# Two sums of a Strassen group, from VectorE additions to adding transfers

## The chip, the core and the metric

The kernel runs on one core of a Trainium2 chip. A core has TensorE (matrix products; PE and, for its weight loads, PEld in the profile), VectorE (DVE), ScalarE (ACT), GpSimd (POOL) and SyncE (SP), each with its own queue of instructions worked off in order, and DMA transfers that engines issue and that then run by themselves. Two kinds matter here: loads issued from SP, and loads and adding transfers issued from POOL. An adding transfer reads one region and adds it onto another where that lies. The metric is the device time of the launch in microseconds (us).

## The reference

One block of an encoder on 256 rows of 2048 numbers, in float32: a gated feed-forward part, an attention and a retention mixer side by side, a second feed-forward part, a last normalisation. The change lies in the first feed-forward part:

```python
def rmsnorm(x, g):
    y = xf * lax.rsqrt(jnp.mean(xf * xf, axis=-1, keepdims=True) + EPS)
    return (y * g.astype(jnp.float32)).astype(x.dtype)

def swiglu_ffn(x, w_gate, w_up, w_down):
    return (jax.nn.silu(x @ w_gate) * (x @ w_up)) @ w_down

x = x + 0.5 * swiglu_ffn(rmsnorm(x, norm_ffn1_g[l]), ffn1_w_gate[l], ffn1_w_up[l], ffn1_w_down[l])
...
x = x + merged @ w_out[l]
x = x + 0.5 * swiglu_ffn(rmsnorm(x, norm_ffn2_g[l]), ffn2_w_gate[l], ffn2_w_up[l], ffn2_w_down[l])
return rmsnorm(x, norm_final_g)
```

The gate and up matrices are 2048 x 5632, the down matrix 5632 x 2048.

## The kernel before

**Products.** Every float32 factor is split into a high part and a low remainder, and a product is three matrix products: high by high, high weight by low activation, low weight by high activation. A chunk of weights is 256 rows by 512 columns, 128 partitions by 1024 numbers. `split` (lines 132 to 136) makes its halves: ScalarE copies it to the high half (L134), VectorE subtracts that from the chunk for the low half (L135). `three` issues the products at L145, L146 (with the high half) and L148 (with the low half). Four split chunks can be alive at a time, and five raw ones.

**Strassen groups.** The gate and up products of one block of 512 columns are made together, as a two by two block product with seven products of sums in place of eight (class `Strassen`, L524). Each group is named after the entry at which it begins: `z10` is the first one, `z46` the second. It works on four chunks `jc` = 0 to 3 in four phases. For the first phase it loads, over POOL's queue, tiles `z10k` (up) and `z10x` (gate) for each chunk (`go`, L552). The plain halves `hiz1000r` to `loz1003r` are split from `z10k`; then the *first sum* of each chunk, `x = x + k`, is made and split into `hiz1000s` to `loz1003s`. In a name like `loz1003s` the last digits are the phase (0), the chunk (3), and `r` for a plain chunk or `s` for a sum. The second phase adds a further raw chunk onto `x` (L608), splits the sum, then forms `k = x - k` (L593) and lets an adding transfer put another chunk onto `x` (`third`, L594).

**Who makes the first sums.** `first` (L541) does it on VectorE, in place. For chunks named in `group.added`, `add_on` (L557) issues an adding transfer from `k` onto `x` on POOL's queue instead, `add_wait` entries after the chunk's second load. `weave` (L698) gives each group `group.added = group.added[:n]` with `n` its number in its part: none for group 0, chunk 0 for group 1, chunks 0 and 1 for the later ones.

**The order of the work.** The program is a written list of entries, each one chunk or a pair of a plain chunk and a sum; `run` walks it, preparing chunks some entries ahead. `later(n, ...)` puts something n entries behind. `kept.extend` (L729) releases the eight loads of the first group one entry apart. All of it is fixed when the program is built: on each engine the instructions stand in one order, and each waits for what it reads.

**The start.** The first ten entries ahead of `z10` are ordinary gate and up chunks (`acc`, names `hi`, `lo`, `raw`). While they run, VectorE and ScalarE also form the sums of the normalised activations that the groups need (`n1s5`, `n1s6`, `n1s3`, `n1s7`; L494 to L508), and ScalarE the squares of the norm (`n1sq`, L436). The norm's factor `n1rstd` (L383) is made on POOL.

Of the kernel before, what the change touches and what calls it, by code (L numbers as in the profile page):

```python
# [41 lines left out]
RET_WAIT = (14, 5)  # L42
HELD = 6
MIX_ADDED = (0,)
HEAD_AT = (3, 6, 10, 13, 17, 20, 24, 27)

MIX_SHARE = (0.5,) * 4 + (1.0,) * 4 + (0.0,) * 4 + (0.2,) * 4
# [33 lines left out]
def block_kernel(ctx: ExitStack, tc: tile.TileContext, x, g1, w1g, w1u, w1d, gm, w_in, rel, woa, wor, wo,  # L81
# [32 lines left out]
    def later(n, fn):  # L114
        due.setdefault(state["step"] + n, []).append(fn)
# [34 lines left out]
    def standard(job, k0):  # L150

        made = {}
        c = len(steps)

        parts = [slice(j, j + 1) for j in range(KC)] if c == 0 else [slice(0, KC)]

        def load():
            made["raw"] = weights_tile(f"raw{c}")
            fetch(made["raw"], job.w, job.rows[k0], job.col0, parts)

        def prep():
            if c > 0:
                made["hl"] = split(made.pop("raw"), c)
                return

            hi, lo = made["hl"] = split_tiles(c)
            raw = made.pop("raw")
            for p in parts:
                nc.vector.tensor_copy(hi[:, p, :], raw[:, p, :])
            first_low.extend(lambda p=p: nc.vector.tensor_sub(lo[:, p, :], raw[:, p, :], hi[:, p, :].bitcast(F32)) for p in parts)  # L170

        def products(only=None):
            if k0 == 0 and only in (None, 0) and not job.seed:
                open_banks(job)
            hi, lo = made["hl"]
            turns = [
                [
                    (
                        job.acc[part], job.act(k0 + j, t), (hi[:, j, cs], lo[:, j, cs]),
                        k0 + j == 0 and not job.seed, k0 + j == job.nk - 1,  # L180
                    )
                    for j in range(KC)
                ]
                for part, (t, cs) in enumerate(job.parts) if only in (None, part)
            ]

            if 0 < k0 < job.nk - KC:
                turns = [sum(turns, [])]
            for products in turns:
                three(products, bool(job.seed))  # L190
            if only is None and k0 + KC == job.nk:
                close(job)

        return Step(job, k0, load, prep, ("raw",), products)
# [503 lines left out]
    def weave(jobs, apart, groups, lead, share, start=None, extra=0):  # L698


        queue = [(job, k) for job in jobs for k in range(0, job.nk, KC)]
        at_hand = {}

        def next_standard():

            if len(queue) <= apart:
                return False
            job, k = queue[0]
            if any(at_hand.get(b, len(steps) + 1) > len(steps) for b in job.needs):
                return False  # L710
            steps.append(standard(job, k))
            del queue[0]
            if job.makes is not None and k + KC == job.nk:
                at_hand[job.makes] = len(steps) + 9
            return True

        for _ in range(lead):
            next_standard()
        seconds = []
        rate = (len(queue) - apart) / (len(groups) * sum(share))  # L720
        credit = 0.0
        first = max(len(steps) - 8, D // NB)
        for n, (b, make) in enumerate(groups.items()):
            group = make()
            group.added = group.added[:n]
            loads = group.loads()
            if start is not None and n == 0:
                loads[0] = lambda load=loads[0]: [start(), load()]
            kept.extend((first + i if n == 0 else 0, fn) for i, fn in enumerate(loads))  # L729
            for i, part in enumerate(group.steps()):  # L730
                if i == HALF_K // KC + 2:
                    seconds.append(len(steps))
                steps.extend(part)
                credit += rate * share[i]
                if i + 1 == len(share):
                    at_hand[b] = len(steps) + 7

                turn = i + 1 == 3 * (HALF_K // KC)
                if (turn or credit >= (0.2 if (i + 1) % (HALF_K // KC) == 0 else 0.6)) and next_standard():
                    credit -= 1  # L740
        if extra:
            due.setdefault(seconds[0], []).append(lambda: room.update(kept=room["kept"] + extra))
            due.setdefault(len(steps), []).append(lambda: room.update(kept=room["kept"] - extra))
        for job, k in queue:
            steps.append(standard(job, k))

    def ffn(name, norm, wg, wu, wd, after, start=None):
# [83 lines left out]
        for job, follow in zip(jobs, jobs[1:]):  # L831
            job.next = follow
        groups = {b: (lambda b=b: paired(b)) for b in range(nblocks) if b != PLAIN}
        weave(jobs, len(downs[PASSES[-1]]) * len(PASSES[-1]) * 4 // KC + HELD, groups, LEAD[start is None], SHARE, start, EXTRA)


# [169 lines left out]
    def all_attention():  # L1006
        for h in range(HEADS):
            for s, stage in attention(h):
                later(HEAD_AT[h] + s, stage)

# [67 lines left out]
    def gates(col1, col2, func, dsts):  # L1078
# [9 lines left out]

        return Strassen(nm, w_in0, col1, w_in0, col2, evict, MIX_ADDED)

# [6 lines left out]
    def queries():  # L1097
# [9 lines left out]

        return Strassen(nm, w_in0, QA, w_in0, QA + NB, evict, MIX_ADDED)

    groups = {"qa": queries, **groups}  # L1110
    weave(
        [proj(KA + b * NB, att_qk_done("ka", b), both) for b in range(2)]
        + [proj(VA + b * NB, nat_done("va", b, AF.Copy), both) for b in range(2)]
# [215 lines left out]
```

## Time and profile before

| | before |
|---|---|
| median of 3 runs | 2052.51 us (2051.78 to 2052.53) |
| the profiled execution, its own time | 2052.5 us |
| its span | 2050.7 us |
| PE busy | 2033.1 us (99%) |
| PEld busy | 1678.2 us (82%) |
| DVE busy | 1789.2 us (87%) |
| ACT busy | 1499.5 us (73%) |
| POOL busy | 343.8 us (17%) |
| granted TensorE clock, mean | 0.999 |

1.8 us of the profiled execution lie outside its span. PE's busy time comes from modelled ends of pipelined products, so gaps are better read from the weight loads (PEld): each product needs one, and where a load waits, a bracket behind its row says how long the engine was idle and for whom.

### The profile page before, as it was taken

Reading aid. Unit: us, or ns where it says so; the run is one execution under the profiler, and the core shown is the slowest. Engines: PE = TensorE matmul, PEld = TensorE weight load, DVE = VectorE, ACT = ScalarE, POOL = GpSimd, SP = SyncE. Lnnn points to the kernel's source line nnn. Section 1 sums busy time; section 2 is a strip of 40 time slices with the busy share of each in tenths; the row PEclk is TensorE's granted clock in tenths of the full one; section 3 lists DMA queues with packets and bytes.
Section 4 is the critical chain, followed back from the end, with each engine's and each line's share of the span. In section 5 each row is a group of like instructions: output and inputs, shape, how many; then the busy total and the mean of one; then the engine's idle time right before and its main releaser. Section 6 shows DMA issues by size and latency. Waiting matters only on the chain.

```text
span 2050.7 us, 26315 instructions
## 1 busy us (share of the span) xinstructions
PE 2033.1 (99%) x9188; PEld 1678.2 (82%) x9188; DVE 1789.2 (87%) x1837; ACT 1499.5 (73%) x1890; POOL 343.8 (17%) x403
## 2 busy tenths in 40 slices
PE   9999999999999999999999999999999999999998
PEld 7788888888888878888888888888788888888886
DVE  7999999999998799999987667569989999989996
ACT  7788888878787767777775434556788788888785
POOL 1221122212112022112120000011212221112200
PEclk9999999999999999999999999999999999999999
DMA  8888889988878679899896645576989988889974
GB/s 289 246 249 259 253 269 283 260 243 246 262 233 270 223 214 300 280 280 286 251 324 221 222 139 190 185 241 187 271 263 270 275 245 234 268 258 269 277 205 134
DMA packets 226853, 506.33 MB, mean 247 GB/s; under 512 B 15824, under 2 KB 16576, under 8 KB 226720
## 3 DMA queue, kind: packets, MB, share of 16 engines
q1 hardware_dynamic: 154560, 297.31, 43.1%
q0 software_dynamic: 67952, 198.36, 37.0%
q10 hardware_dynamic: 4208, 8.99, 1.2%
q8 instruction: 72, 1.18, 0.2%
q14 instruction: 61, 0.50, 0.1%
HBM read 472.08 MB, written 12.06 MB: 236 GB/s over the span
## 4 chain that ended last, share of the span: by engine, by line
PE 93%; DVE 3%; DMA 2%; ACT 1%; issue 1%; POOL 0%; SPq 0%; DVEq 0%; POOLq 0%; ACTq 0%
PE acc L148 15%; PE acc L145 15%; PE acc L146 15%; DMA z1030k<-in_ffn_w_up_dram 1%; DMA raw<-in_ffn_w_gate_dram 1%; DMA z1030x<-z1030k 1%; DVE lo L135 1%; PE z425a L145 0%; PE z777a L145 0%; PE z704a L146 0%; PE z958a L145 0%; PE z262a L145 0%; PE z190a L145 0%; PE z425a L146 0%; PE z226a L146 0%
## 5 line engine op out<-in xcount | busy, mean ns | idle before, releaser
L135 DVE TENSOR_TENSOR lo<-raw,hi 128x1024 fp32r<-128x1024 f32 x351 | 427.0, 1219 | 118.0 <-ACT hi L134 115.2
L134 ACT CAST hi<-raw 128x1024 fp32r<-128x1024 f32 x351 | 367.7, 1050 | 161.0 <-PE acc L146 125.7
L817 ACT ACTIVATE xall<-acc 128x512 f32<-128x512 f32 x160 | 94.5, 590 | 13.6 <-PE acc L148 9.7
L814 ACT ACTIVATE acc<-xall 128x512 f32<-128x512 f32 x160 | 95.9, 599 | 2.5
L145 PE MATMUL acc<-hi,mgh 128*128 128x512 f32 x128 | 50.2, 392 | 0.0
L146 PE MATMUL acc<-hi,mgl 128*128 128x512 f32 x128 | 49.8, 389 | 0.0
L148 PE MATMUL acc<-lo,mgh 128*128 128x512 f32 x128 | 35.5, 389 | 0.0
L145 PE MATMUL acc<-hi,nma01h 128*128 128x512 f32 x80 | 32.5, 407 | 0.0
L145 PE MATMUL acc<-hi,nma00h 128*128 128x512 f32 x80 | 32.3, 404 | 0.0
L146 PE MATMUL acc<-hi,nma01l 128*128 128x512 f32 x80 | 31.3, 391 | 0.0
L146 PE MATMUL acc<-hi,nma11l 128*128 128x512 f32 x80 | 31.3, 391 | 0.0
L146 PE MATMUL acc<-hi,nma00l 128*128 128x512 f32 x80 | 31.2, 390 | 0.0
L145 PE MATMUL acc<-hi,nma11h 128*128 128x512 f32 x80 | 31.2, 390 | 0.0
L146 PE MATMUL acc<-hi,nma10l 128*128 128x512 f32 x80 | 31.2, 390 | 0.0
L145 PE MATMUL acc<-hi,nma10h 128*128 128x512 f32 x80 | 31.2, 390 | 0.0
L148 PEld LDWEIGHTS acc<-lo,mgh 128*128 128x128 f32 x128 | 24.0, 188 | 5.0
L145 PEld LDWEIGHTS acc<-hi,mgh 128*128 128x128 f32 x128 | 24.0, 188 | 4.9
L146 PEld LDWEIGHTS acc<-hi,mgl 128*128 128x128 f32 x128 | 24.0, 188 | 4.8
L145 PE MATMUL acc<-hi,atth 128*128 128x512 f32 x64 | 26.2, 410 | 0.0
L148 PE MATMUL acc<-lo,nma01h 128*128 128x512 f32 x80 | 24.9, 393 | 0.6 <-DVE lo L135 0.6
L145 PE MATMUL acc<-hi,reth 128*128 128x512 f32 x64 | 25.3, 395 | 0.0
L146 PE MATMUL acc<-hi,attl 128*128 128x512 f32 x64 | 25.1, 392 | 0.0
(6884 smaller groups left out, 7258.8 us busy)
## 6 DMA issues: line engine op xcount, KB each, us to landing
raw<-in_ffn_w_down_dram SPq DMA_DIRECT2D x176, 512.0 KB, 6.7
raw<-in_w_in_dram SPq DMA_DIRECT2D x80, 512.0 KB, 5.0
raw<-in_w_out_dram SPq DMA_DIRECT2D x32, 512.0 KB, 4.1
raw<-in_ffn_w_up_dram SPq DMA_DIRECT2D x16, 512.0 KB, 5.0
raw<-in_w_out_att_dram SPq DMA_DIRECT2D x16, 512.0 KB, 4.3
raw<-in_w_out_ret_dram SPq DMA_DIRECT2D x16, 512.0 KB, 3.9
raw<-in_ffn_w_gate_dram SPq DMA_DIRECT2D x15, 512.0 KB, 4.9
z390x<-in_w_in_dram POOLq DMA_DIRECT2D x8, 512.0 KB, 8.7
```

The source lines that it names most:

```text
L134: nc.scalar.copy(hi, raw)
L135: nc.vector.tensor_sub(lo, raw, hi.bitcast(F32))
L145: nc.tensor.matmul(acc, ahi, whi, start=first, stop=False, **more)
L146: nc.tensor.matmul(acc, alo, whi, start=False, stop=False, **more)
L148: nc.tensor.matmul(acc, ahi, wlo, start=False, stop=last, **more)
L814: nc.scalar.activation(acc, xs[t][:, cols], AF.Copy, scale=2.0)
L817: nc.scalar.activation(xs[t][:, cols], acc, AF.Copy, scale=0.5)
```

## The change

The last two first sums of group `z10` are taken from VectorE and made by adding transfers. `add_wait` is set to 2 for this group, so the transfer for a chunk is called for two entries after the chunk's `x` load. The chunks 0 and 1 stay on VectorE. Other groups are as before.

```diff
@@ -42,6 +42,7 @@
 HELD = 6
 MIX_ADDED = (0,)
+FIRST_ADDED = (2, 3)
 HEAD_AT = (3, 6, 10, 13, 17, 20, 24, 27)
@@ -722,7 +723,9 @@
         for n, (b, make) in enumerate(groups.items()):
             group = make()
-            group.added = group.added[:n]
+            group.added = FIRST_ADDED if n == 0 and start is not None else group.added[:n]
+            if n == 0 and start is not None:
+                group.add_wait = 2
             loads = group.loads()
```

Only the first feed-forward part passes a `start`. The new line shifts line numbers by one, and by three from L726 on.

On POOL's queue, at the first group's loads, before (`z10k_435` and `z10x_463` are chunk 2, `z10k_487` and `z10x_503` chunk 3; a name behind the arrow is what is read):

```order
L552 DMA z10k_435<-in_ffn_w_up_dram 128x2x512
L552 DMA z10x_463<-in_ffn_w_gate_dram 128x2x512
L552 DMA z10k_487<-in_ffn_w_up_dram 128x2x512
L552 DMA z10x_503<-in_ffn_w_gate_dram 128x2x512
L383 TENSOR_TENSOR n1rstd<-v,mhalf 128x2
L594 DMA z10x_340<-in_ffn_w_up_dram 128x2x512
```

and after:

```order
L553 DMA z10k_435<-in_ffn_w_up_dram 128x2x512
L553 DMA z10x_463<-in_ffn_w_gate_dram 128x2x512
L553 DMA z10k_487<-in_ffn_w_up_dram 128x2x512
L553 DMA z10x_503<-in_ffn_w_gate_dram 128x2x512
L558 DMA z10x_463<-z10k_435 128x1024
L558 DMA z10x_503<-z10k_487 128x1024
L384 TENSOR_TENSOR n1rstd<-v,mhalf 128x2
L595 DMA z10x_340<-in_ffn_w_up_dram 128x2x512
```

The two adding transfers stand behind all eight loads and ahead of the norm's factor. Both wait there until the two loads of their chunk have landed.

On VectorE, at the plain halves and sums of the first phase, before:

```order
L135 TENSOR_TENSOR loz1002r<-z10k_435,hiz1002r 128x1024
L541 TENSOR_TENSOR z10x_463<-z10x_463,z10k_435 128x1024
L503 TENSOR_TENSOR n1f_258<-n1x_158 128x4x128
L508 TENSOR_TENSOR n1s3l<-n1f_258,n1s3h 128x512
L135 TENSOR_TENSOR loz1001s<-z10x_411,hiz1001s 128x1024
L500 SCALAR_TENSOR_TENSOR n1f_397<-n1f_397,n1x_348 128x4x128
L508 TENSOR_TENSOR n1s6l<-n1f_397,n1s6h 128x512
L135 TENSOR_TENSOR loz1003r<-z10k_487,hiz1003r 128x1024
L541 TENSOR_TENSOR z10x_503<-z10x_503,z10k_487 128x1024
L135 TENSOR_TENSOR lo_559<-raw_325,hi_558 128x1024
L508 TENSOR_TENSOR n1s7l<-n1f_258,n1s7h 128x512
L135 TENSOR_TENSOR loz1002s<-z10x_463,hiz1002s 128x1024
```

and after:

```order
L136 TENSOR_TENSOR loz1002r<-z10k_435,hiz1002r 128x1024
L504 TENSOR_TENSOR n1f_258<-n1x_158 128x4x128
L509 TENSOR_TENSOR n1s3l<-n1f_258,n1s3h 128x512
L136 TENSOR_TENSOR loz1001s<-z10x_411,hiz1001s 128x1024
L501 SCALAR_TENSOR_TENSOR n1f_397<-n1f_397,n1x_348 128x4x128
L509 TENSOR_TENSOR n1s6l<-n1f_397,n1s6h 128x512
L136 TENSOR_TENSOR loz1003r<-z10k_487,hiz1003r 128x1024
L136 TENSOR_TENSOR lo_559<-raw_325,hi_558 128x1024
L509 TENSOR_TENSOR n1s7l<-n1f_258,n1s7h 128x512
L136 TENSOR_TENSOR loz1002s<-z10x_463,hiz1002s 128x1024
```

Two additions are gone and nothing else has moved. TensorE's, ScalarE's and SyncE's rows stand in the same order in both programs; ScalarE's `hiz1002s` and `hiz1003s` now wait for the adding transfers where they waited for VectorE.

## The prediction, as put on record before the changed kernel ran

> **What bounds the kernel now.** I first read the table of busy time by windows of 50 us, over the whole span, to see where TensorE is not full. Columns: window, length, busy us and count for PE, PEld, DVE, ACT, POOL, granted clock, DMA share, GB/s; ahead of it the page's line of busy time.
>
> ```profile
> PE 2033.1 (99%) x9188; PEld 1678.2 (82%) x9188; DVE 1789.2 (87%) x1837; ACT 1499.5 (73%) x1890; POOL 343.8 (17%) x403
> 0.00:50.00 50.00, 48.13 (x213) 37.93 (x214) 37.17 (x47) 39.05 (x70) 7.49 (x15) 1.00 0.83 296
> 50.00:100.00 50.00, 47.99 (x208) 37.44 (x208) 49.46 (x52) 35.99 (x44) 14.27 (x16) 1.00 0.83 232
> 100.00:150.00 50.00, 50.00 (x226) 41.45 (x226) 47.59 (x44) 40.42 (x52) 10.93 (x12) 1.00 0.87 250
> 600.00:650.00 50.00, 50.00 (x222) 41.40 (x221) 46.28 (x44) 40.11 (x51) 8.24 (x9) 1.00 0.79 221
> ```
>
> From 100 to 650 us PE is full in every window (the first and the last of eleven are shown). In the window from 50 to 100 us, where group z10 is worked on, PE does 208 products in place of some 226, and VectorE is busy for 49.46 of 50 us. The clock is 1.00, so this is no throttling. Next, the weight loads in time order for that stretch, those rows that carry a wait, and the two loads ahead of the largest.
>
> ```profile
> 49.84 0.30 PEld L148 LDWEIGHTS z10a<-loz1003r,n1a00h 128*128 128x128 f32 x2 [0.20 <-DVE loz1003r L135]
> 54.77 0.19 PEld L145 LDWEIGHTS z10c<-hiz1003s,n1s5h 128*128 128x128 f32 x1
> 55.00 0.19 PEld L146 LDWEIGHTS z10c<-hiz1003s,n1s5l 128*128 128x128 f32 x1
> 56.46 0.30 PEld L148 LDWEIGHTS z10c<-loz1003s,n1s5h 128*128 128x128 f32 x2 [1.27 <-DVE loz1003s L135]
> 73.02 0.30 PEld L148 LDWEIGHTS z10c<-loz1013r,n1s3h 128*128 128x128 f32 x2 [0.31 <-DVE loz1013r L135]
> 75.29 0.30 PEld L148 LDWEIGHTS acc<-lo,n1a01h 128*128 128x128 f32 x2 [1.04 <-DVE lo L135]
> 80.96 0.30 PEld L148 LDWEIGHTS z10b<-loz1020r,n1a01h 128*128 128x128 f32 x2 [0.37 <-DVE loz1020r L135]
> 81.63 0.42 PEld L392 LDWEIGHTS f1a10p<-id_sb,f1g 128*128 128x128 f32 x4 [0.36 <-DVE f1g L781]
> 82.28 0.42 PEld L392 LDWEIGHTS f1a10p<-id_sb,f1g 128*128 128x128 f32 x4 [0.24 <-DVE f1g L781]
> 89.81 0.30 PEld L148 LDWEIGHTS z10b<-loz1023r,n1a01h 128*128 128x128 f32 x2 [0.90 <-DVE loz1023r L135]
> 91.54 0.30 PEld L148 LDWEIGHTS z10a<-loz1022s,n1s7h 128*128 128x128 f32 x2 [0.50 <-DVE loz1022s L135]
> ```
>
> Every one of these waits is for VectorE. Loads follow each other every 0.23 us (54.77, 55.00), 0.04 of it idle, so the nine brackets, 5.19 us together, are about 4.8 us lost (9 x 0.04 taken off). This stage is bound by VectorE; 4.8 us is the most that any cure of it could bring. What VectorE does when the stage begins, by its own rows in time order:
>
> ```profile
> 43.90 1.22 DVE L541 TENSOR_TENSOR z10x<-z10x,z10k 128x1024 f32<-128x1024 f32 x1
> 45.03 0.68 DVE L503 TENSOR_TENSOR n1f<-n1x 128x512 f32<-128x512 f32 x1
> 48.58 1.22 DVE L135 TENSOR_TENSOR loz1003r<-z10k,hiz1003r 128x1024 fp32r<-128x1024 f32 x1
> 49.71 1.21 DVE L541 TENSOR_TENSOR z10x<-z10x,z10k 128x1024 f32<-128x1024 f32 x1
> 50.85 1.22 DVE L135 TENSOR_TENSOR lo<-raw,hi 128x1024 fp32r<-128x1024 f32 x1
> 52.58 1.22 DVE L135 TENSOR_TENSOR loz1002s<-z10x,hiz1002s 128x1024 fp32r<-128x1024 f32 x1
> 55.19 1.22 DVE L135 TENSOR_TENSOR loz1003s<-z10x,hiz1003s 128x1024 fp32r<-128x1024 f32 x1
> ```
>
> None of these seven rows has a bracket: VectorE waited for nothing, it was simply late. The two L541 rows are the additions that the change takes away.
>
> **What is removed.** Instructions overlap slightly, so the price is the distance to the next start: 45.03 - 43.90 = 1.13 us and 50.85 - 49.71 = 1.14 us, together **2.27 us** of VectorE, all spent before `loz1003s`, the half for which PE waits longest.
>
> How far does that reach PE? `loz1003s` can start at 55.19 - 2.27 = 52.92 and end at 54.14 (it takes 1.22). PE would ask for it at 55.00 + 0.23 = 55.23: the gap of 1.23 us closes. So does the one at 49.84 (0.16), as the first addition is gone by then (1.13). PE is then 1.39 us ahead of before. The gap at 73.02 (0.27) needs VectorE earlier by 1.39 + 0.27 = 1.66 of the 2.27, and closes too. The one at 75.29 (1.00) would need 2.66: 0.39 of it stays. From here PE is ahead by exactly what VectorE is, 2.27 us, and the later gaps stay as they are, since PE, VectorE and what they release all stand 2.27 us earlier. After 92 us PE has no gaps for 550 us, so the lead is carried on, and nothing behind depends on the clock time at which it began.
>
> This needs ScalarE to be early enough, for it makes each high half first. Its rows:
>
> ```profile
> 49.03 1.05 ACT L134 CAST hiz1002s<-z10x 128x1024 fp32r<-128x1024 f32 x1
> 51.01 1.06 ACT L134 CAST hiz1003s<-z10x 128x1024 fp32r<-128x1024 f32 x1 [0.31 <-DVE z10x L541]
> 54.70 0.62 ACT L507 CAST n1s7h<-n1f 128x512 fp32r<-128x512 f32 x1 [1.17 <-DVE n1f L503]
> 74.21 1.05 ACT L134 CAST hiz1013s<-z10x 128x1024 fp32r<-128x1024 f32 x1 [3.16 <-DVE z10x L608]
> ```
>
> `hiz1002s` ends at 50.08; VectorE would want it at 52.58 - 2.27 = 50.31. That is close, 0.2 us, but enough. `hiz1003s` loses its wait of 0.31 and ends at 51.76, 1.2 us ahead of need. Later ScalarE is the one that waits (1.17, 3.16 us), and for VectorE, so it moves along. I let ScalarE cost nothing; were the 0.2 us of cover gone, it costs what is missing, once.
>
> **What is added.** Two issues on POOL and two adding transfers of 512 KB. The issues cost no path anything: POOL has nothing to do between the last load and `n1rstd` at 54 us. Behind the two waits stands only `n1rstd`, which waits for VectorE. The price of the transfers is their landing, since `hiz1002s` and `hiz1003s` stand in ScalarE's queue with everything else behind them. First the loads on which they wait, from the lists of DMA issues around 24.5 and 26 us (last number: us from issue to landing) with POOL's issues in time order, then the adding transfers that the program has already, all 38 of L557 (their count by the waits ahead of them; then least, median, most), and the DMA engines around that time, with the columns of the first table.
>
> ```profile
> 24.49 0.74 POOL L552 DMA_DIRECT2D z10x<-in_ffn_w_gate_dram  x1
> z10x<-in_ffn_w_gate_dram POOLq DMA_DIRECT2D x1, 512.0 KB, 13.7
> 25.92 0.75 POOL L552 DMA_DIRECT2D z10x<-in_ffn_w_gate_dram  x1
> z10x<-in_ffn_w_gate_dram POOLq DMA_DIRECT2D x1, 512.0 KB, 16.4
> 54.16 1.09 POOL L383 TENSOR_TENSOR n1rstd<-v,mhalf 128x2 f32<-128x2 f32 x1 [27.49 <-DVE v L382]
> L557 POOLq EVENT_SEMAPHORE  x38: 17/43/16957, 89.6 to 1888.7; - x38
> DMA to landing us min/median/max: 4.6/6.9/11.9
> L557 POOL DMA_DIRECT2D z82x<-z82k x2: 921/924/927, 115.0 to 159.1; - x2
> 40.00:41.00 1.00, 1.00 (x6) 0.84 (x5) 1.00 (x2) 1.00 (x4) 0.00 (x0) 1.00 1.01 375
> 43.00:44.00 1.00, 1.00 (x6) 0.82 (x5) 1.00 (x2) 1.00 (x2) 0.00 (x0) 1.00 0.74 279
> 44.00:45.00 1.00, 1.00 (x6) 0.83 (x5) 1.00 (x1) 1.00 (x4) 0.00 (x0) 1.00 0.00 0
> 49.00:50.00 1.00, 1.00 (x6) 0.72 (x5) 1.00 (x2) 1.00 (x3) 0.00 (x0) 1.00 0.00 0
> ```
>
> Chunk 2 is complete at 24.49 + 13.7 = 38.2, chunk 3 at 25.92 + 16.4 = 42.3. The adding transfers, issued then, land at 38.2 + 4.6 to 11.9 = 42.8 to 50.1 and at 42.3 + 4.6 to 11.9 = 46.9 to 54.2. They are wanted by ScalarE at 49.03 and, with its wait gone, at 50.70. By the median of 6.9 they land at 45.1 and 49.2, early by 3.9 and 1.5 us. I take the median or less for chunk 3: from 44 to 50 us the DMA engines had nothing to do, while most of the 38 run among loads. Chunk 2's starts in the busy stretch that ends at 44 us, and even at 10 us it is in time. The idle engines are also why I charge nothing for loads that the new transfers push back.
>
> How late is too late: `loz1003s` starts no earlier than the landing plus 1.06. Up to a landing at 52.92 - 1.06 = 51.9 nothing is lost; at 54.1 (55.19 - 1.06) the gain is used up; the longest of the 38 would give 54.2, no gain.
>
> **Sum.** -1.13 - 1.14 + 0 + 0 = -2.27 us. Against the profiled execution, 2052.5 (span 2050.7 and 1.8 around it), that is 2050.2; the median of the runs, 2052.51, is the same to 0.01, so the forecast is **2050.3**. By the bounds of the landing it runs from -2.27 to +0.05.
>
> **The rivals.**
>
> *The gain stops early.* ScalarE's high halves, or the four places for split chunks, hold VectorE once it is ahead, and PE keeps only the two gaps up to 57 us: 1.39, hence 2051.1. For it speaks the cover of 0.2 us at `hiz1002s`; against it that ScalarE is idle for 14 of the 50 us and mostly waits for VectorE there.
>
> *Nothing is gained.* The transfers land around 54 us, or the lead is swallowed by a wait that the trace of before can't show: 2052.5. For it: the longest landing, 11.9. Against: idle DMA engines.
>
> *Late, and in series.* The second transfer goes through the same queue as the first and begins only when that has landed, both among loads. At 10 us each (38.2 + 20) it lands at 58.2, which is 58.2 + 1.06 - 55.19 = 4.1 us later than `loz1003s` starts today, with VectorE and ScalarE waiting in order behind it: 2056.6. It decides from a landing at 54.1 on. Against it: two of 6.9 in series end at 52.0, in time but for 0.1 us.
>
> [...]
>
> **Chances.** Forecast 0.66; gain stops early 0.14; nothing gained 0.11; late in series 0.04; held back 0.02; something else in either direction 0.03. A measurement of this kernel can tell about 0.2%, 4.1 us, from no change. The forecast, the early stop and no gain all lie within that; only the two late rivals lie at it or beyond, and beyond it on the other side lies only a cure of nearly all 4.8 us, for which 2.27 us of VectorE are too few. So: faster 0.03, same 0.92, slower 0.05. The range for 8 in 10 holds the first three cases with 0.4 us for the spread of the runs: 2049.6 to 2052.9.
>
> **What would show it.** In the new trace: no L541 row at 43.90 and 49.71; `loz1003s` starts near 52.9; PEld has no wait for it; the PEld wait near 73 us shrinks from 1.04 to about 0.4; PE does about 218 products from 50 to 100 us; the adding transfers land before 49 and 50.7, ScalarE's `hiz1002s` and `hiz1003s` carry no bracket for them. I am wrong if `hiz1003s` waits for a DMA beyond 52 us, if PE's gaps come back at other rows so that they still sum to 4.8, or if the lead is there at 100 us and gone at 650.

## The result, and the profile after

The change runs in 2049.73 us (median of 20 runs, 2048.88 to 2051.47), the kernel before beside it in 2052.52 us (20 runs, 2051.18 to 2053.80): 2.79 us less, a ratio of 0.9987 with a 95% interval of 0.9981 to 0.9993. The forecast was 2050.3 us and a gain below what can be told from no change (0.2%); the interval is clear of 1 all the same, so 20 runs of each kernel can tell a smaller change than 0.2%. The profiled execution took 2049.28 us, its span 2047.5.

First the table by windows for the stretch in which the change lies (columns as in the prediction), and the weight loads in time order between 44 and 95 us, all rows that carry a wait.

```profile
50.00:100.00 50.00, 49.45 (x218) 39.41 (x217) 48.96 (x51) 38.10 (x47) 14.25 (x16) 1.00 0.87 250
```

```profile
73.20 0.30 PEld L149 LDWEIGHTS acc<-lo,n1a01h 128*128 128x128 f32 x2 [0.28 <-DVE lo L136]
...
78.88 0.30 PEld L149 LDWEIGHTS z10b<-loz1020r,n1a01h 128*128 128x128 f32 x2 [0.34 <-DVE loz1020r L136]
79.54 0.42 PEld L393 LDWEIGHTS f1a10p<-id_sb,f1g 128*128 128x128 f32 x4 [0.36 <-DVE f1g L784]
80.20 0.42 PEld L393 LDWEIGHTS f1a10p<-id_sb,f1g 128*128 128x128 f32 x4 [0.24 <-DVE f1g L784]
...
87.73 0.30 PEld L149 LDWEIGHTS z10b<-loz1023r,n1a01h 128*128 128x128 f32 x2 [0.91 <-DVE loz1023r L136]
88.20 0.19 PEld L146 LDWEIGHTS z10a<-hiz1022s,n1s7h 128*128 128x128 f32 x1 [0.17 <-ACT hiz1022s L135]
...
89.46 0.30 PEld L149 LDWEIGHTS z10a<-loz1022s,n1s7h 128*128 128x128 f32 x2 [0.51 <-DVE loz1022s L136]
```

PE now does 218 products in the window where it did 208. The waits for `loz1003r`, `loz1003s` and `loz1013r` are gone (0.20, 1.27 and 0.31 us before), the one for `lo` went from 1.04 to 0.28, and the others stand as they were, 2 us earlier. VectorE is still busy for 48.96 of the 50 us, and six of the seven waits that are left are for it: it still bounds the stage.

VectorE and then ScalarE in time order, the rows that answer to those of the prediction:

```profile
42.92 1.23 DVE L136 TENSOR_TENSOR loz1002r<-z10k,hiz1002r 128x1024 fp32r<-128x1024 f32 x1
...
47.60 1.23 DVE L136 TENSOR_TENSOR loz1003r<-z10k,hiz1003r 128x1024 fp32r<-128x1024 f32 x1
...
50.47 1.23 DVE L136 TENSOR_TENSOR loz1002s<-z10x,hiz1002s 128x1024 fp32r<-128x1024 f32 x1
51.61 0.17 DVE L443 TENSOR_REDUCE tot<-n1ss 128x2 f32<-128x8 f32 x1
...
53.09 1.22 DVE L136 TENSOR_TENSOR loz1003s<-z10x,hiz1003s 128x1024 fp32r<-128x1024 f32 x1
```

```profile
49.19 1.05 ACT L135 CAST hiz1002s<-z10x 128x1024 fp32r<-128x1024 f32 x1
...
50.76 1.05 ACT L135 CAST hiz1003s<-z10x 128x1024 fp32r<-128x1024 f32 x1
```

Neither row of ScalarE has a bracket: the transfers were there in time. Their issues on POOL, then how long each took to land (from the lists of DMA issues around 38 and 42 us, last number, us), and the DMA engines just behind:

```profile
38.18 0.94 POOL L558 DMA_DIRECT2D z10x<-z10k  x1 [11.40 <-DMA z10x<-in_ffn_w_gate_dram]
42.26 0.86 POOL L558 DMA_DIRECT2D z10x<-z10k  x1 [3.13 <-DMA z10x<-in_ffn_w_gate_dram]
```

```profile
z10x<-z10k POOLq DMA_DIRECT2D x1, 512.0 KB, 6.9
...
z10x<-z10k POOLq DMA_DIRECT2D x1, 512.0 KB, 6.7
```

```profile
44.00:45.00 1.00, 1.00 (x6) 0.84 (x5) 1.00 (x3) 1.00 (x3) 0.00 (x0) 1.00 1.07 338
...
48.00:49.00 1.00, 1.00 (x6) 0.81 (x5) 1.00 (x2) 1.00 (x4) 0.00 (x0) 1.00 0.07 12
```

Chunk 2's sum is there at 45.1 us and chunk 3's at 49.0, wanted at 49.19 and 50.76. The four microseconds from 44 to 48 in which the DMA engines had nothing to do before (a share of 0.00 in each) now go to the sums: 1.07, 1.14, 0.99 and 0.51.

### The profile page after: what moved, and what is told of

It reads as the page before. It is cut to its first block, busy times and chain, and to the rows that moved or that the text cites. A ratio compares the mean times of both kernels' runs of the same rounds, so it can differ in the third digit from the quotient of the medians.

```text
span 2047.5 us, 26319 instructions
## 1 busy us (share of the span) xinstructions
PE 2032.2 (99%) x9188; PEld 1679.2 (82%) x9188; DVE 1786.8 (87%) x1835; ACT 1500.0 (73%) x1890; POOL 345.6 (17%) x405
## 4 chain that ended last, share of the span: by engine, by line
PE 95%; DMA 2%; DVE 2%; ACT 1%; issue 1%; POOL 0%; DVEq 0%; POOLq 0%; ACTq 0%
PE acc L149 15%; PE acc L146 15%; PE acc L147 15%; DMA z1030k<-in_ffn_w_up_dram 1%; DMA z1030x<-z1030k 1%; DMA raw<-in_ffn_w_gate_dram 0%; PE z425a L146 0%; PE z425a L147 0%; PE z190a L146 0%; PE z262a L146 0%; PE z777a L146 0%; PE z704a L147 0%; PE z226a L147 0%; PE z154a L147 0%; PE z922a L146 0%
```

## A measure that isolates the stage

The medians scatter by about half a microsecond, and an execution starts some tenths earlier or later. The stage itself can be measured within one trace: from the start of `loz1000r`, ahead of everything that the change touches, to the start of `loz1033s`, the last low half of group z10. Before, and then after:

```profile
33.12 1.22 DVE L135 TENSOR_TENSOR loz1000r<-z10k,hiz1000r 128x1024 fp32r<-128x1024 f32 x1
...
99.47 1.22 DVE L135 TENSOR_TENSOR loz1033s<-z10x,hiz1033s 128x1024 fp32r<-128x1024 f32 x1
```

```profile
33.30 1.22 DVE L136 TENSOR_TENSOR loz1000r<-z10k,hiz1000r 128x1024 fp32r<-128x1024 f32 x1
...
97.39 1.23 DVE L136 TENSOR_TENSOR loz1033s<-z10x,hiz1033s 128x1024 fp32r<-128x1024 f32 x1
```

That is 66.35 us before and 64.09 after: 2.26 less, where the sum of the prediction was 2.27. This length, read from the same two rows of each experiment's trace, beside the difference of the medians (the kernel's less that of the kernel before in the same session):

| kernel | stage, us | against before | medians | ratio, 95% interval |
|---|---|---|---|---|
| before | 66.35 | | | |
| the change | 64.09 | -2.26 | -2.79 | 0.9987 [0.9981, 0.9993] |
| the change, again | 64.10 | -2.25 | -1.97 | 0.9988 [0.9979, 0.9997] |
| chunk 3 alone | 65.22 | -1.13 | -1.84 | 0.9993 [0.9984, 1.0002] |
| no sums at all | 64.09 | -2.26 | -2.53 | 0.9989 [0.9980, 0.9998] |
| chunks 1, 2 and 3 | 65.22 | -1.13 | -1.03 | 0.9996 [0.9987, 1.0005] |
| two subtractions doubled | 68.87 | +2.52 | +2.48 | 1.0013 [1.0005, 1.0022] |
| late, POOL multiplies after `loz1001s` | 69.22 | +2.87 | +3.14 | 1.0015 [1.0006, 1.0024] |
| late, POOL multiplies after `loz1003r` | 69.48 | +3.13 | +3.40 | 1.0014 [1.0005, 1.0022] |
| late, small transfer after `loz1001s` | 65.57 | -0.78 | -1.11 | 0.9995 [0.9986, 1.0004] |
| late, small transfer after `loz1003r` | 70.35 | +4.00 | +3.45 | 1.0016 [1.0007, 1.0024] |
| change in all three first groups | 64.06 | -2.29 | -5.72 | 0.9972 [0.9961, 0.9983] |

One of the eleven runs of "chunk 3 alone" took 9526.89 us; its median is that of the other ten. Where only this stage was altered, medians and stage differ by at most 0.7 us, in both directions. Each length is read from one trace; the kernels that leave VectorE's work in this stage as the change has it, with transfers in time or none, read 64.06 to 64.10.

## The experiments

The theory: the stage is bound by VectorE, so VectorE's time taken out comes out of the end one for one, and the transfers cost nothing as long as they land in time. The rivals: the gain has another source or stops early; the transfers take something back; a late landing costs more, or less, than the prediction has it.

**Chunk 3 alone.** One addition goes back to VectorE.

```
-FIRST_ADDED = (2, 3)
+FIRST_ADDED = (3,)
```

> Only chunk 3's first sum is an adding transfer; chunk 2's stays on VectorE. Theory V (TensorE waits for VectorE from 46 to 92 us, and each VectorE instruction taken out ahead of loz1003s moves everything behind it by its distance to the next start): 1.14 us of VectorE are gone, so loz1003s starts at about 54.05 and the time falls by 1.1 us (2051.4), half of the change's forecast. Rival T (the adding transfers, or what their traffic shifts, bring or cost something of their own beside the VectorE time, which would explain why the change measured 2.79 and not 2.27): the fall is not 1.1 but about 1.6 or more. Rival S (ScalarE's queue decides): nearly nothing.

The stage is 1.13 us shorter, which is half of the change's 2.26. The term of each addition is confirmed. The medians fell by 1.84 and not by 1.1, which by itself would speak for rival T; they can't decide it, as their interval runs from a gain of 0.16% to a loss of 0.02%. What decides is where the rest lies: it isn't in the stage, and the next kernel, which has no such transfers at all, also has medians that fall by more than its stage.

**No sums at all.** The sums of chunks 2 and 3 are left out altogether, by VectorE and by transfer: part of the computation is missing here.

```
-                    nc.gpsimd.dma_start(self.x[jc], self.kept[jc], accum_op=ALU.add)
+                    if self.added is not FIRST_ADDED:
+                        nc.gpsimd.dma_start(self.x[jc], self.kept[jc], accum_op=ALU.add)
```

> The first sums of chunks 2 and 3 of group z10 are left out altogether, on VectorE and as transfers, so x stays the bare gate chunk there and the result is another one; all other work is the same. Theory V: the transfers are hidden and cost nothing, so this is as fast as the change: VectorE's loz1003s starts within 0.1 us of the changed kernel's 53.09, the lead at 100 us is the same, the time falls by 2.3 us against the kernel before. Rival T: if the transfers cost something, it is faster than the changed kernel by that (0.5 us or more); if their traffic is what brought the 0.5 beyond 2.27, it falls by 2.3 where the change falls by 2.8.

64.09 us, the same as the change. The two transfers of 512 KB cost this stage nothing that can be seen, and they bring nothing; the change gets all that taking away the two additions can bring.

**Three chunks.** Chunk 1's sum becomes a transfer too, issued four entries behind its load.

```
-FIRST_ADDED = (2, 3)
+FIRST_ADDED = (1, 2, 3)
-                    later(self.add_wait, lambda: add_on(jc))
+                    later(4 if self.added is FIRST_ADDED and jc == 1 else self.add_wait, lambda: add_on(jc))
```

> Chunk 1's first sum is an adding transfer too, issued behind all eight loads and ahead of those of chunks 2 and 3. It frees a third 1.14 us of VectorE. Theory V with ScalarE's cover of 0.2 us at hiz1002s: VectorE can't start loz1002s before hiz1002s ends (50.2 in the changed kernel's trace), where it would be ready at 49.3; so of the third 1.14 us only 0.2 to 0.3 are kept and the fall against the kernel before is 2.5 us, if chunk 1's transfer lands by 43.4, when ScalarE wants hiz1001s (issued at about 34, so it needs 9.4 or less; the 38 of the trace take 4.6 to 11.9). If it lands later, ScalarE, which has no idle time from 39 to 52 us, is late by as much, and the fall is 2.27 less that lateness. Rival (VectorE alone decides): the fall is 3.4 us.

Worse than two chunks by 1.13 us. The issue for chunk 1, its landing, ScalarE's row behind it, and a row of VectorE ahead of it:

```profile
33.31 0.94 POOL L558 DMA_DIRECT2D z10x<-z10k  x1 [7.19 <-DMA z10x<-in_ffn_w_gate_dram]
```

```profile
z10x<-z10k POOLq DMA_DIRECT2D x1, 512.0 KB, 10.7
```

```profile
44.13 1.05 ACT L135 CAST hiz1001s<-z10x 128x1024 fp32r<-128x1024 f32 x1 [1.24 <-DMA z10x<-z10k]
```

```profile
41.78 1.23 DVE L136 TENSOR_TENSOR loz1002r<-z10k,hiz1002r 128x1024 fp32r<-128x1024 f32 x1 [0.57 <-ACT hiz1002r L135]
```

Issued among loads (from 33.0 to 34.5 us POOL's queue has 64.7% of the DMA engines and SP's 38.1%), this transfer takes 10.7 us and lands at 44.0, and ScalarE waits 1.24 us for it. The third addition saved would have brought 1.13, but it can't be used: VectorE, now earlier, waits 0.57 us for ScalarE's `hiz1002r` (the last row) even before that landing. ScalarE works without a pause there (in the trace of the change its rows follow each other without a bracket from 39.3 to 56.1 us). Without the wait it would have begun `hiz1001s` at 44.13 - 1.24 = 42.89, 10.26 us behind the start of `loz1000r`; in the change that is 10.16, so the third addition does not make ScalarE any earlier. So this kernel gains what the change gains, less the wait: 2.26 - 1.24 = 1.02, and 1.13 was measured. By this reckoning two chunks are about as many as ScalarE lets VectorE use; a third transfer that lands in time was not run.

**Two subtractions doubled.** The kernel before, with `loz1002r` and `loz1003r` computed twice, at the places where the change took work out. The result is the same.

```
+                        if self.name == "z10" and jc in (2, 3):
+                            hi, lo = made["w"]
+                            nc.vector.tensor_sub(lo, self.kept[jc], hi.bitcast(F32))
```

> The kernel before, with two VectorE instructions more: the subtractions for loz1002r and loz1003r are each done twice (same result, same size as an addition, 1.13 us each), right ahead of the two additions. Theory V: the slope is one for one in this direction too: 2.27 us slower (2054.8), the wait of TensorE's weight load for loz1003s grows from 1.27 to about 3.5 us. Rival: half or less of it, if other limits share the stage with VectorE; or more, if the doubling delays the loads that wait for VectorE to free buffers.

VectorE at the first of them, and PE's longest wait:

```profile
42.85 1.22 DVE L135 TENSOR_TENSOR loz1002r<-z10k,hiz1002r 128x1024 fp32r<-128x1024 f32 x1
44.10 1.23 DVE L603 TENSOR_TENSOR loz1002r<-z10k,hiz1002r 128x1024 fp32r<-128x1024 f32 x1
45.25 1.22 DVE L541 TENSOR_TENSOR z10x<-z10x,z10k 128x1024 f32<-128x1024 f32 x1
```

```profile
52.45 0.30 PEld L148 LDWEIGHTS z10a<-loz1003r,n1a00h 128*128 128x128 f32 x2 [2.37 <-DVE loz1003r L603]
```

From `loz1002r` to the addition behind it VectorE takes 45.25 - 42.85 = 2.40 us where it took 1.13 or 1.14, so 1.26 more, and 2.53 for both. The stage is 2.52 longer. One for one in this direction too. The wait for `loz1003s` did not grow to 3.5 us, as was expected: PE's longest wait moves from `loz1003s` to `loz1003r` (2.37), as the second repeat makes that half late.

**The landing made late, behind an operation of POOL.** In two kernels the transfer for chunk 3 stands behind a small POOL multiplication (128x4) that reads `loz1001s`, or `loz1003r`, so that it is issued later.

```
+                    if behind is not None:
+                        gate = small.tile([P, NB // P], F32, tag="behind", name="behind", bufs=1)
+                        nc.gpsimd.tensor_tensor(gate, behind[:, 0, : NB // P].bitcast(F32), mhalf, op=ALU.mult)
                     nc.gpsimd.dma_start(self.x[jc], self.kept[jc], accum_op=ALU.add)
...
-                if jc in self.added:
+                if jc in self.added and not (self.added is FIRST_ADDED and jc == 3):
...
+                    if self.added is FIRST_ADDED and phase == 0 and jc == 1:
+                        self.add_on(3, made["w"][1])
```

These lines are those of the first of the two; in the second, the call stands behind `loz1003r` in the same way.

> As the changed kernel, but POOL issues chunk 3's adding transfer only when VectorE has made loz1001s (a small POOL operation ahead of the issue reads it). In the changed kernel's trace that is ready at 46.5; the operation takes some 0.8, so the issue starts at about 47.3 and, on idle DMA engines, lands 4.6 to 6.9 us later, at about 53 (51.9 to 54.2). The prediction's tolerance (nothing lost up to a landing at 51.9, everything at 54.1, one for one between) then gives: ScalarE's hiz1003s carries a wait for the transfer, loz1003s starts 1.06 after the landing, at about 54.1 in place of 53.1, and the fall against the kernel before shrinks from 2.27 to about 1.2 us (0.1 to 2.3 over the landings' range, by the landing that the trace shows). Rival (VectorE or ScalarE have other work to put in between): the fall stays at 2.27.

> The same with loz1003r in place of loz1001s, ready at 48.8 in the changed kernel's trace: issue at about 49.7, landing at about 55.4 (54.3 to 56.6). By the tolerance the gain is gone and the change is slower than the kernel before, one for one: loz1003s starts at about 56.5, where the kernel before starts it at 55.19, so about 1.2 us slower than before (0 to 2.3 by the landing). Rival: no slower than before, as TensorE has other products to do.

Both landed equally late and both missed their expectations: the first was to be 1.2 us faster than before and its stage is 2.87 longer, the second was to be 1.2 slower, 2.3 at most, and its stage is 3.13 longer. POOL in time order in the first, VectorE's row at which POOL went on, and then POOL in the second:

```profile
46.52 5.18 POOL L560 TENSOR_TENSOR behind<-loz1001s,mhalf 128x4 f32<-128x4 f32 x1 [6.73 <-DVE loz1001s L136]
51.65 0.88 POOL L561 DMA_DIRECT2D z10x<-z10k  x1
```

```profile
51.56 0.16 DVE L443 TENSOR_REDUCE tot<-n1ss 128x2 f32<-128x8 f32 x1
```

```profile
48.74 2.85 POOL L560 TENSOR_TENSOR behind<-loz1003r,mhalf 128x4 f32<-128x4 f32 x1 [9.40 <-DVE loz1003r L136]
```

The multiplication of 512 numbers took 5.18 us in one kernel and 2.85 in the other, where the same operation on a tile of that size (L844, at 19.95 us in the kernel before) takes 0.80, and ended at 51.70 and 51.59, whenever it began: just after VectorE's first instruction with a single tensor as input (the `TENSOR_REDUCE` at 51.56, and at 51.44 in the second). Ahead of that VectorE runs nothing but instructions that read two tensors, one right behind the other: six of them from 46.34 us on beside the first multiplication, three from 48.57 on beside the second. The operation meant to set the time of the issue was itself late. That VectorE held it up is the author's estimate from these two ends, 0.14 and 0.15 us behind the start of that row; no run shows it by itself.

**The same with a gate that POOL doesn't compute.** The multiplication is replaced by a very small transfer, in both kernels.

```
-                        nc.gpsimd.tensor_tensor(gate, behind[:, 0, : NB // P].bitcast(F32), mhalf, op=ALU.mult)
+                        nc.gpsimd.dma_start(gate, behind[:, 0, : NB // P].bitcast(F32))
```

> As the first late run, but POOL's second transfer is put behind a very small transfer (128 x 4 of loz1001s into a small tile) in place of POOL's own multiplication. Theory (what stood still was POOL's own reading of SBUF; the issue of a transfer doesn't stand still): the small transfer is issued when loz1001s ends, about 46.4 us, takes POOL about 0.9, the adding transfer is issued at 47.3 and lands 4.8 to 6.9 later, at 52.1 to 54.2; loz1003s starts 1.15 behind it, at 53.3 to 55.4 (52.9 in the change, 55.2 before). VectorE ends up 1.9 earlier to 0.2 later than before, ScalarE's late queue takes up to 0.5 of it: 2050.2 to 2052.8 where the kernel before has 2052.3, middle 2051.3. Rival (POOL's whole queue stands still while VectorE reads two tiles without a pause, issues too): issue at 51.6, landing past 56, 2055.2 as in the first late run.

> As the second late run, with the same small transfer (of loz1003r) as the gate. Theory: small transfer at 48.7, adding transfer issued at 49.7, landing 54.5 to 56.6, past the point of 54.1 to 54.7 at which the gain is used up; loz1003s starts 55.7 to 57.8, 0.5 to 2.6 later than before, and ScalarE's late queue adds about 0.5: 2053.3 to 2055.4 where the kernel before has 2052.3. Beside the first of this pair it tells whether lateness of landing costs one for one from about 52 us on. Rival (issues stand still too): issue at 51.5, landing 56.5, 2055.4, the same as in the first of the pair.

POOL, ScalarE and VectorE in the first, then POOL and ScalarE in the second:

```profile
46.70 0.56 POOL L560 DMA_DIRECT2D behind<-loz1001s  x1 [7.59 <-DVE loz1001s L136]
47.25 0.90 POOL L561 DMA_DIRECT2D z10x<-z10k  x1
```

```profile
52.79 1.05 ACT L135 CAST hiz1003s<-z10x 128x1024 fp32r<-128x1024 f32 x1 [1.99 <-DMA z10x<-z10k]
```

```profile
53.87 1.23 DVE L136 TENSOR_TENSOR loz1003s<-z10x,hiz1003s 128x1024 fp32r<-128x1024 f32 x1 [0.78 <-ACT hiz1003s L135]
...
55.33 1.23 DVE L136 TENSOR_TENSOR lo<-raw,hi 128x1024 fp32r<-128x1024 f32 x1 [0.16 <-ACT hi L135]
56.80 1.23 DVE L136 TENSOR_TENSOR loz1010r<-rawz1010r,hiz1010r 128x1024 fp32r<-128x1024 f32 x1 [0.24 <-ACT hiz1010r L135]
```

```profile
49.39 0.90 POOL L561 DMA_DIRECT2D z10x<-z10k  x1
```

```profile
57.42 1.04 ACT L135 CAST hiz1003s<-z10x 128x1024 fp32r<-128x1024 f32 x1 [6.82 <-DMA z10x<-z10k]
```

Two things follow. Issues were not held: 0.56 and 0.90 us, amid the same VectorE work. That it was POOL's own reading that stood still, as the theory of the first of this pair has it, isn't shown by that: what the traces show is a multiplication of 5.18 and 2.85 us, and issues of 0.56 and 0.90. The second kernel's time, 2055.68, lies above its expectation and close to the 2055.4 of the rival with held issues; what tells them apart is the row of its issue, at 49.39 and not at 51.5, so it was the landing that took longer than expected (8.0 us), not the issue. And there is now a curve of lateness. Start of `hiz1003s`, put on the clock of the trace of before by the start of `loz1000r`, and the stage against before:

| `hiz1003s` starts | stage against before |
|---|---|
| 50.58 (the change) | -2.26 |
| 52.71 (small transfer, first) | -0.78 |
| 56.37 (multiplication, first) | +2.87 |
| 56.63 (multiplication, second) | +3.13 |
| 57.51 (small transfer, second) | +4.00 |

The last four lie on a line of slope one (56.37 - 52.71 = 3.66 for 3.65; 57.51 - 56.37 = 1.14 for 1.13). It reaches zero at 53.49 and, drawn on, -2.26 at 51.23 (no kernel has a late landing between 50.58 and 52.71). By this line nothing is lost up to a landing at about 51.2 us, at about 53.5 the gain is used up; ScalarE's cast begins within 0.1 us of the landing (in the first kernel with the multiplication at 56.49, where 51.65 + 4.8 is 56.45). The second of this pair lands 8.0 us after its issue and the first 5.5. In the second a load of 512 KB (`rawz1012r`) was issued 0.3 us behind the transfer and took 7.8 us, in the first 2.7 us behind it and 5.5, where the kernel before and the change have 3.6 and 4.4 for that load. So both took longer in the kernel in which they were issued closer together. That the two share the DMA engines is the author's estimate from these times; no run sets them apart.

**All three first groups.** The change in the first group of each of the program's three parts with such sums (z10, z390 of the mixers, z704 of the second feed-forward part).

```
-            group.added = FIRST_ADDED if n == 0 and start is not None else group.added[:n]
-            if n == 0 and start is not None:
+            group.added = FIRST_ADDED if n == 0 else group.added[:n]
+            if n == 0:
```

> The change made in all three places where a part begins with a first group: group z10 as in the changed kernel, group z390 of the mixers' input products, and group z704 of the second feed-forward part, chunks 2 and 3 each. Theory V: at z390 TensorE's weight loads wait 5.5 us in total for VectorE or what follows it (2.25 of it for loz39002s, which starts behind both additions), so 2.27 us are gained there; at z704 VectorE waits for ScalarE until 1391 us and TensorE's waits behind it sum to little: 0.3 to 0.9. Together with z10's 2.27: 4.8 to 5.4 us less than the kernel before (2047.2 to 2047.8), 2.6 to 3.2 less than the change. Rival: z390's transfers land late among the loads there (chunk 3 is complete at 711.7 us; ScalarE's hiz39003s is wanted at about 718) and z390 gives under 1 us.

2046.38 us (median of 7 runs, 2045.78 to 2047.16) against 2052.10: faster than before and than the change (2050.13 beside it), and 0.3 us more than the 4.8 to 5.4 that was expected. PE's largest wait for VectorE in group z390, 690 to 770 us (us in total, times, longest), before and here; then around z704, 1340 to 1470 us, those two of before that are gone here, and all that is left here:

```profile
PEld z390c L148 <- DVE loz39002s L135: 2.2, 1, 2.2
```

```profile
PEld z390c L149 <- DVE loz39002s L136: 1.1, 1, 1.1
```

```profile
PEld z740a L148 <- DVE loz74002r L135: 1.0, 1, 1.0
...
PEld z704a L148 <- DVE loz70413s L135: 0.2, 1, 0.2
```

```profile
PEld f2a0p L393 <- PE f2a0p L393: 0.7, 1, 0.7
PEld acc L149 <- DVE lo L136: 0.6, 1, 0.6
```

In z390 the length from `loz39000r` to `loz39033s` falls from 62.69 to 60.41, by 2.28, as in z10. In z704 VectorE also gets 2.27 ahead by the end of the first phase (`loz70400r` to `loz70403s`: 22.02, now 19.75), but up to `loz70433s` only 1.36 is left (65.14, now 63.78): the waits of PE for VectorE that could go there were only 1.2 us (1.0 + 0.2 in the rows above), and once they are gone PE sets the pace. 2.29 + 2.28 + 1.2 = 5.8 against the 5.72 of the medians. That this fits to 0.1 is partly luck. Kernels that leave z390 as it was read 62.10 to 62.94 for its length, and in those that leave z704 as it was PE's wait for `loz74002r` is anything from 0.34 to 1.11 us, so that the share of z704 can be 0.5 as well as 1.2.

**The change again**, unaltered, in the second session.

> The changed kernel itself once more, beside the others. Theory V: the lead over the kernel before is 2.27 us from 55 to 700 us, as in its first trace, and what its first profiled execution gained beyond that (0.66 us at 1440 us, where ScalarE waits for the landing of a raw load, and some 0.3 later) comes and goes between executions: the fall of the medians is 2.3 to 2.8, and the step at 1440 us differs from 0.66 in this trace. Rival T: the same steps at the same places, and 2.8 again.

The stage is 64.10 us, the median 1.97 below before in place of 2.79, and a little less than the 2.3 to 2.8 that was expected. What differs lies elsewhere: from `loz70400r` to `loz70433s`, where every kernel but the one with three groups has the same instructions, traces read 65.14 (before), 64.47 (the change), 64.78 (the change again), 64.70 (no sums), 65.34 (small transfer, first) and 65.77 (three chunks). One part of that is a landing. ScalarE in the trace of before and of the change:

```profile
1436.16 1.06 ACT L134 CAST hi<-raw 128x1024 fp32r<-128x1024 f32 x1 [1.12 <-DMA raw<-in_ffn_w_up_dram]
```

```profile
1432.99 1.06 ACT L135 CAST hi<-raw 128x1024 fp32r<-128x1024 f32 x1 [0.17 <-DMA raw<-in_ffn_w_up_dram]
```

This wait is 1.33 in the trace of the first small transfer, 0.68 without sums, and absent in the change again. PE's wait for `loz74002r` just behind it is 1.03 before, 0.34 in the change and 0.66 in the change again. Both are a matter of the execution more than of the change.

## Why the prediction was right

**What bounds the stage.** Right, and now shown in both directions: 2.26 us of the stage for 2.27 of VectorE taken out, 1.13 for one addition, 2.52 for 2.53 put in.

**The gaps.** Right, row by row: those at 49.84, 56.46 and 73.02 us closed, the one at 75.29 was to keep 0.4 and kept 0.28, the later ones stayed, and PE does the 218 products that were named. The prediction's list of nine waits, all for VectorE, left out a tenth in that stretch, a short one for ScalarE:

```profile
90.28 0.19 PEld L145 LDWEIGHTS z10a<-hiz1022s,n1s7h 128*128 128x128 f32 x1 [0.17 <-ACT hiz1022s L134]
```

It stands in the new list too (88.20), so nothing hangs on it. The seven brackets left sum to 2.81 us; with 0.04 taken off each that is 2.53, against 5.36 - 0.40 = 4.96 for the ten of before: 2.43 less, where the stage is 2.26 shorter; the brackets are the coarser measure of the two.

**ScalarE's cover.** `hiz1002s` ends at 50.24 and `loz1002s` starts at 50.47, with no bracket. The cover of 0.2 us was enough, and the rival that the gain stops early falls.

**The landings.** 6.9 and 6.7 us, where the median of the 38 transfers was 6.9; 7.2 and 6.5 in the change again, 7.8 and 7.2 in the kernel with three groups. So three traces of the same pair land in time, and the good landing was no luck of one execution. That they cost the stage nothing is shown by the kernel without them (64.09 us with and without). In the kernel before the DMA engines are idle from 44 to 50 us (0.00), but the pair was no faster for it than the median. Chunk 3's transfer starts at 42.26, while chunk 2's is under way to 45.1; with no other sum under way it took from 4.8 us (behind the first multiplication) to 8.0 (behind the second small transfer), and in the kernel with three, beside loads and the other sums, 9.1 (chunk 1's 10.7). These times alone don't show what made a transfer slow.

**The lead is carried on.** `loz39000r` starts 2.04 us earlier than before at 707 us (2.22 with the later start of this execution taken off), and `loz70400r` 2.22 at 1379 (2.40 in the same way).

**What failed: how late is too late.** The prediction had nothing lost up to a landing at 51.9, the gain used up at 54.1, from the step "`loz1003s` starts no earlier than the landing plus 1.06". The line above gives about 51.2 and 53.5. The step looked at `loz1003s` alone. ScalarE's casts queue behind `hiz1003s`, and with that late VectorE waits for the next two as well (0.16 and 0.24 in the rows of the first small transfer). `loz1003s` itself started 1.40 us earlier there than before, on the common clock, and 0.78 was left at the end of the stage: 0.6 us is lost behind it. The trace of the change shows how little room there is, at the third cast behind `hiz1003s`:

```profile
53.69 1.06 ACT L135 CAST hiz1010r<-rawz1010r 128x1024 fp32r<-128x1024 f32 x1
```

```profile
55.43 1.22 DVE L136 TENSOR_TENSOR loz1010r<-rawz1010r,hiz1010r 128x1024 fp32r<-128x1024 f32 x1
```

`hiz1010r` ends at 54.75 and VectorE takes it up at 55.43, 0.68 us later; `hiz1003s` ends at 51.81 and `loz1003s` starts at 53.09, 1.28 later. From the cast's start at 50.58 in the table, 0.68 us of room reach to 51.26, where the line gave 51.23. The landing at 49.0 was early by 2 us even so, which is why the forecast did not suffer from this step.

**The held issue.** "Held back" had 0.02 of the chances. Issues of adding transfers took 0.86 to 0.94 us in the very stretch in which VectorE works without a pause (0.94 and 0.86 in the change, 0.90 in both kernels with the small transfer), and 0.92 in the kernel before: they were not held. The multiplication beside the same work took 5.18 and 2.85 us; why it did and the issues didn't is not shown.

**The number.** 2050.3 was forecast and 2049.73 measured; the other session gave 2050.13. The stage accounts for 2.26 of the 2.79. The rest is of the size by which the medians of these kernels stand off their stage in either direction (at most 0.7), and lies in places that vary from one execution to the next, PE's wait for `loz74002r` the largest that was found; its cause isn't settled. The measured time lies near the lower end of the range (2049.6), which allowed for a smaller gain and for the spread of the runs but hardly for a larger gain.

## What to carry to other kernels

Where a busy engine is seen as the last one waited for in a stage, price a removal by the start-to-start distance of its instructions, and follow which of the gaps of the engine behind it are still fed by that lead: a group where those gaps sum to 1.2 us can't pay back 2.3. For a transfer that takes over such work, look for a stretch in which the DMA engines are idle (here 6.9 and 6.7 us for the two that reach into one, 10.7 for one that was issued among loads), and set the latest landing not by the first instruction that needs it but by the whole queue behind that instruction. A tiny operation on POOL was no safe way to time a transfer here: the multiplication of 128x4 numbers took 5.18 and 2.85 us in place of 0.80, where the small transfer was issued in 0.56.

## What the runs showed of the hardware

A POOL multiplication of 128x4 numbers took 5.18 and 2.85 us (0.80 elsewhere in the kernel before) while VectorE ran instructions with two tensors as input back to back, and ended 0.14 and 0.15 us after the start of the first VectorE instruction with one. It lasted over six such VectorE instructions in the one kernel and over three in the other; what made it last is not shown. DMA issues on POOL in the same stretch took 0.56 to 0.94 us.

In the kernel that landed latest (second small transfer) PE had no product from 54.5 to 58.5 us. Its granted clock by windows of 1 us (third number from the end):

```profile
56.00:57.00 1.00, 0.00 (x0) 0.00 (x0) 0.00 (x0) 0.00 (x0) 0.00 (x0) 0.96 0.07 14
57.00:58.00 1.00, 0.00 (x0) 0.00 (x0) 0.00 (x0) 0.58 (x1) 0.00 (x0) 0.50 0.01 4
...
62.00:63.00 1.00, 1.00 (x4) 0.71 (x4) 1.00 (x2) 1.00 (x3) 0.00 (x0) 0.50 0.60 104
63.00:64.00 1.00, 1.00 (x4) 0.80 (x3) 1.00 (x2) 0.85 (x1) 0.00 (x0) 0.63 0.96 350
```

The granted clock is 1.00 up to 56 us, 0.96 from 56 to 57, 0.50 in each window from 57 to 63, 0.63 from 63 to 64, and 1.00 behind that. If it was either full or half, these means put the fall at 56.9, about 2.4 us into the pause, and the return at 63.7, nearly 7 us later and more than 5 us after PE was at work again: an estimate from this one trace. In the windows at 0.50 from 59 us on PE did 4 products in a microsecond in place of 6. Yet this kernel lies on the same line of lateness as the others (+4.00 at 57.51), and PE's first wait for VectorE comes back only at 85.5 us; that PE caught up in the gaps that it otherwise has in this stage is the author's estimate from these two figures.
